# A two-layer decoder trunk in float32: the compressed branch's second products and two activation-table loads are issued elsewhere

## The chip, the cores and the metric

The kernel runs on one core of one Trainium2 chip. The metric is device time in microseconds (us) of one launch; the kernel before took 1310.82 us (median of three runs, 1310.17 to 1310.92). The core has five engines that work side by side, each through a queue of its own and in order: TensorE (PE in the profile; its weight loads are PEld), VectorE (DVE), ScalarE (ACT), GpSimd (POOL) and SyncE (SP), which here only issues DMAs.

## The reference, cut to what matters

Two layers, 512 tokens, width 1024, all float32. Layer 0 mixes by two linear recurrences, layer 1 by sparse attention with three branches; a SwiGLU network follows each. What the change touches is the compressed branch of layer 1 and the SiLU of the network:

```python
def compress_blocks(k, pos_emb, w1, w2):          # k: 512 tokens, 2 groups, 64 wide
    blocks = windows_of_32_tokens_every_16(k) + pos_emb      # 31 blocks
    return jax.nn.silu(blocks.reshape(..., 32 * 64) @ w1) @ w2   # 31 x 64 per group

def odd_mixer(h, ...):
    q, kc, vc, ks, vs, kw, vw, gl = split_cols(h @ w_in, ODD_COLS)
    k_cmp, v_cmp = compress_blocks(kc, ...), compress_blocks(vc, ...)
    # per head: softmax over k_cmp, over selected blocks and over a window;
    # the three outputs are mixed by sigmoid(gl), then h + out @ w_out

def swiglu(h, w_gate_up, w_down):
    g, u = jnp.split(h @ w_gate_up, 2, axis=-1)
    return (jax.nn.silu(g) * u) @ w_down
```

## The kernel before

Activations lie transposed: 8 tiles of 128 features by 512 tokens. Every large product is made of three matmuls (`mm3`, L89 to L91): operands are cut into a high part (a cast on ACT, L78: `wh`) and a low part (a subtraction, L79: `wl`, on DVE, or on POOL for the query weights). Weights come by DMA on SP's queue into `raw`, three buffers, in program order.

The program is written as a list of steps, and a scheduler with a simulated timeline turns it into one order for each engine; it keeps data dependences and buffer reuse, and moves instructions freely otherwise. `tc.issue_after(x)` tells it not to issue a step before instruction `x`; `tc.keep_in_program_order` keeps a step in its place among the others of its engine. The orders are fixed at build time: on the chip each engine takes its own strictly in turn and waits where an input is missing.

The stages that matter here, in order of time:

1. **The end of a layer's network** (`ffn`, L321 to L361). The hidden rows are made in groups of 2, 4, 4, 4, 4, 4. Each hidden tile goes through a SiLU on ACT (L343), a product on DVE (L344), and is cut into `hh` (ACT, L347) and `hl` (DVE, L348). Behind the loop ACT is told to load the table set that has both exp and ln (L355); then the last group's down projections follow.
2. **The head of layer 1** (`odd`, L705 on). Four projections (`proj`, tiles `ps_o`), the row norm (`row_rstd`: a matmul `ps_n`, then Ln on L127, Exp on L128, and three DVE steps L129 to L131), then for keys and values of the compressed branch `compress`: four DVE copies spread the projected tile `z` into `cx` (L832), eight fp32 matmuls with `w1` give `ps_c` (L837; the profile counts two passes for each), a short chain on ACT and DVE makes a SiLU out of exp, ln and exp (`sigmoid`, L152 to L156; result `cu`, L850), and the second product with `w2` gives `ps_c2` (L853 for keys, L858 for values). In the profile `ps_c` names both. Keys end up in `kc`, values in `vc`. The 96 matmuls of 304 columns into `ps_v` make the token-major values and the gates.
3. **Four query tiles** (`query_tile`, L782), 24 matmuls each into `ps_q`, scaled on DVE into `qz` (L798); then the attention loop, which first reads `kc` in `ps_cs` (L989).
4. **The head of layer 1's network**, the same code as stage 1 with `row_rstd` in the first hidden tile, and **the end** (`finish`): the final norm in two halves of 256 tokens, each with Ln and Exp (`rstd`), DVE products and output DMAs.

PSUM banks of tag `pt` go round in a ring of three: the first two projections, each `ps_c`, each `ps_c2` and the four early `ps_q` take them in program order.

Of the kernel before, what the change touches and what calls it, by code (L numbers as in the profile page):

```python
# [9 lines left out]
F32 = mybir.dt.float32  # L10
F32R = mybir.dt.float32r
U8 = mybir.dt.uint8
AF = mybir.ActivationFunctionType
# [23 lines left out]
AHEAD = 4  # L37
# [15 lines left out]
class Core:  # L53
# [216 lines left out]
    def ffn(self, outs, w_out, gain, layer, next_gain):  # L270
        tc, nc, io, sp = self.tc, self.nc, self.io, self.sp
        with tc.tile_pool(name="fs", bufs=1) as fs, tc.tile_pool(name="fps", bufs=6, space=PSUM) as fps:
            self.fs = fs
            acc = sp.tile([P, T], F32, tag="acc", name="acc", bufs=1)
            b = {i: [] for i in range(1, 8)}
            kept = []
            for i, m in enumerate(OUT_ORDER):
                ps = self.bank(self.turn + 1 + i // 3, "ps_o") if i in BANK_OUT else \
                    fps.tile([P, T], F32, tag="gu", name="ps_o")
                w = self.weight(w_out[m])  # L280
                if i == BANK_OUT[1] and self.last is not None:
                    with tc.issue_after(self.last):
                        self.dense_t(ps, w, outs)
                else:
                    self.dense_t(ps, w, outs)
                nc.vector.tensor_tensor(self.h[m], ps, self.h[m], ALU.add)
                self.token_side(m, gain, kept, b)
                self.square(m, self.h[m], acc)

            def product(i, a, ps=None):  # L290

                new = ps is None
                if new:
                    ps = fps.tile([P, T], F32, tag="gu", name=f"p{i}")[:, :TH]
                ah, al = a[i]
                for k, (bh, bl) in enumerate(b[i]):
                    c = slice(k * P, (k + 1) * P)
                    self.mm3(ps, ah[:, c], al[:, c], bh, bl, new and k == 0, k == 3, not new)
                return ps

            r = None
            out = []

            def down(hid, first, ms, last):

                nonlocal acc
                for m in ms:
                    ps = fps.tile([P, T], F32, tag="gu", name="ps_d") if last and m in OWN_DOWN else self.bank(m, "ps_d")
                    self.dense_t(ps, self.weight(io["dn"][layer, m, :, P * first:P * (first + len(hid))]), hid)
                    if last:  # L310
                        out.append(self.residual(m, ps, next_gain, acc))
                    else:
                        nc.vector.tensor_tensor(self.h[m], ps, self.h[m], ALU.add)  # L313


            before, first, done = None, 0, 0
            for size in GROUPS:
                hid = []
                for j in range(done, done + size):
                    a = self.weight_side(j, layer)  # L320
                    g = fs.tile([P, T], F32, tag="g", name="g", bufs=2)  # L321
                    s = fs.tile([P, T], F32, tag="s", name="s", bufs=2)
                    c1, c2, c3 = [fs.tile([P, TH], F32, tag="u", name="u", bufs=4) for _ in range(3)]


                    x = product(1, a)
                    nc.scalar.copy(c1, x)
                    y = product(5, a)
                    product(6, a, x)
                    nc.scalar.copy(c2, x)  # L330
                    nc.vector.tensor_tensor(g[:, :TH], product(2, a), c1, ALU.add)
                    if r is None:
                        r = self.row_rstd(acc, self.bank(1, "ps_n"))
                    product(7, a, x)
                    nc.scalar.copy(c3, x)
                    nc.vector.tensor_tensor(s[:, TH:], y, c3, ALU.add)  # L336
                    product(3, a, y)
                    nc.vector.tensor_tensor(g[:, TH:], y, c2, ALU.add)  # L338
                    product(4, a, x)
                    nc.vector.tensor_tensor(s[:, :TH], x, r[:, :TH], ALU.mult)  # L340
                    nc.gpsimd.tensor_tensor(s[:, TH:], s[:, TH:], r[:, TH:], ALU.mult)  # L341
                    (nc.vector if j == NF - 1 else nc.gpsimd).tensor_tensor(g, g, r, ALU.mult)  # L342
                    nc.scalar.activation(g, g, AF.Silu)  # L343
                    nc.vector.tensor_tensor(g, s, g, ALU.mult)  # L344
                    hh = sp.tile([P, T], F32R, tag="xh", name="hh", bufs=8)
                    hl = sp.tile([P, T], F32R, tag="xl", name="hl", bufs=8)
                    nc.scalar.copy(hh, g)  # L347
                    nc.vector.tensor_tensor(hl, g, hh.bitcast(F32), ALU.subtract)  # L348
                    hid.append((hh, hl))
                    if before:  # L350
                        n = KD // size
                        down(before, first, range((j - done) * n, (j - done + 1) * n), False)
                before, first = hid, done
                done += size
            tc.keep_in_program_order(nc.scalar.preload_act_table_set("natural_log_exp_and_others"))  # L355
            if next_gain is None:
                self.finish(hid, [io["dn"][layer, m, :, P * first:] for m in range(KD)], fps)
                return None, None
            acc = sp.tile([P, T], F32, tag="acc", name="acc", bufs=1)
            down(hid, first, range(KD), True)  # L360
            return out, acc  # L361
# [341 lines left out]
    def odd(self, xs, acc):  # L703
        tc, nc, io, sp = self.tc, self.nc, self.io, self.sp
        with tc.tile_pool(name="os", bufs=1) as os_, tc.tile_pool(name="ops", bufs=2, space=PSUM) as op:  # L705
# [3 lines left out]
            kc = os_.tile([P, 64], F32, name="kc")  # L709
# [16 lines left out]
            with tc.tile_pool(name="oe", bufs=1) as oe:  # L726
                self.oe = oe
                w1 = [oe.tile([P, 8, P], F32, tag="w1", name="w1", bufs=2) for _ in range(2)]
                w2 = oe.tile([64, 2, 64], F32, name="w2")
                for i in range(2):  # L730
                    nc.sync.dma_start(w1[i], io["w1"][i])
                nc.sync.dma_start(w2, io["w2"])
# [2 lines left out]
                r = self.row_rstd(acc, pn)  # L735
                pss += [proj(2), proj(3)]
                rt = self.token_rstd(r, op.tile([P, T], F32, tag="po", name="ps_rt", bufs=1))
                for col, ps in enumerate(pss):
                    z = oe.tile([P, T], F32, tag="z", name="z", bufs=3)
                    nc.vector.tensor_tensor(z, ps, r, ALU.mult)  # L740
                    if col < 2:
                        self.compress(col == 1, z, w1[col], w2, kc, vc)
                    else:
                        for g in range(2):
                            self.keys(z, g, *[a[:, col - 2] for a in kk[g]])
# [27 lines left out]
            with tc.tile_pool(name="ol", bufs=1) as ol_:  # L773
# [10 lines left out]
                def query_tile(step, late=True):  # L784

                    raw = raws.popleft()
                    w = self.split(raw, WN, True)
                    query_load()
                    yield
                    ps = self.bank(0, "ps_q") if late else op.tile([P, T], F32, tag="pt", name="ps_q", bufs=3)  # L790
                    for k, (xh, xl) in enumerate(xs):
                        wh, wl = w[k // 4]
                        c = slice(k % 4 * P, k % 4 * P + P)
                        self.mm3(ps, wh[:, c], wl[:, c], xh, xl, k == 0, k == 7)
                        if k % step == step - 1:
                            yield
                    z = ol_.tile([P, T], F32, tag="qz", name="qz", bufs=9)
                    nc.vector.scalar_tensor_tensor(z, ps, 0.125, r, ALU.mult, ALU.mult)  # L798
                    qz.append(z)
                    yield  # L800

                for _ in range(2):
                    query_load()
                for _ in range(AHEAD):
                    for _ in query_tile(1, False):
                        pass
                self.attention(qz, outs, kk, kc, vt, vc, v3, gates, query_tile)
                for i, o in enumerate(outs):
                    oh = sp.tile([P, T], F32R, tag="xh", name="oh", bufs=8)
# [12 lines left out]
        for o in (slice(0, 64), slice(64, P)):  # L822
            nc.vector.tensor_tensor(kl[o], z[own], kh.bitcast(F32)[own], ALU.subtract)

    def compress(self, is_v, z, w1, w2, kc, vc):
        nc, os_, op = self.nc, self.os, self.op
        i = int(is_v)
        x = self.oe.tile([P, 8, 66], F32, tag="cx", name="cx", bufs=1)
# [8 lines left out]
            nc.tensor.matmul(ps[:, :66], w1[:, m], x[:, m], start=m == 0, stop=m == 7)  # L837
        hi = os_.tile([64, 66], F32, tag="chi", name="chi", bufs=1)
        pc = os_.tile([64, 1], F32, tag="cpc", name="cpc", bufs=1)
        u = os_.tile([64, 2, 31], F32, tag="cu", name="cu", bufs=1)  # L840
        e = os_.tile([64, 2, 31], F32, tag="ce", name="ce", bufs=1)
        s = os_.tile([64, 2, 31], F32, tag="cs", name="cs", bufs=1)
        n = os_.tile([64, 2, 31], F32, tag="cn", name="cn", bufs=1)
# [4 lines left out]
        nc.vector.tensor_scalar(n, u, -1.0, None, ALU.mult)  # L848
        self.sigmoid(s, n, e)
        nc.vector.tensor_tensor(u, u, s, ALU.mult)  # L850
        ps2 = op.tile([P, T], F32, tag="pt", name="ps_c2", bufs=3)
        if not is_v:
            nc.tensor.matmul(ps2[:64, :62], w2[:, 0], u.rearrange("p g c -> p (g c)"), start=True, stop=True)  # L853
# [307 lines left out]
```

## Time and profile before

| | |
|---|---|
| median of the runs | 1310.82 us |
| the profiled execution's own time | 1311.86 us |
| its span, first to last instruction | 1308.9 us |
| PE busy | 1270.2 us (97%) |
| DVE, ACT, POOL busy | 79%, 56%, 25% |
| DMA | 115.10 MB, mean 88 GB/s |
| TensorE clock granted, mean | 0.984 of full |

How to read it: with PE at 97%, what can be gained lies where PE stands idle or runs at the lower clock. The profile's list of waits names these places, the timeline of one engine shows them in order, and the busy time by stretch gives the granted clock (1.00 is full, 0.50 is the lower level). A matmul's own duration includes its drain; the distance from one start to the next is its price in a row of matmuls.

### The profile page before, as it was taken

Reading aid. Unit: us, or ns where it says so; the run is one execution under the profiler, and the core shown is the slowest. Engines: PE = TensorE matmul, PEld = TensorE weight load, DVE = VectorE, ACT = ScalarE, POOL = GpSimd, SP = SyncE. Lnnn points to the kernel's source line nnn. Section 1 sums busy time; section 2 is a strip of 40 time slices with the busy share of each in tenths; the row PEclk is TensorE's granted clock in tenths of the full one; section 3 lists DMA queues with packets and bytes.
Section 4 is the critical chain, followed back from the end, with each engine's and each line's share of the span. In section 5 each row is a group of like instructions: output and inputs, shape, how many; then the busy total and the mean of one; then the engine's idle time right before and its main releaser. Section 6 shows DMA issues by size and latency. Waiting matters only on the chain.

```text
span 1308.9 us, 21707 instructions
## 1 busy us (share of the span) xinstructions
PE 1270.2 (97%) x7846; PEld 1120.7 (86%) x7846; DVE 1028.2 (79%) x2027; ACT 731.7 (56%) x1587; POOL 332.0 (25%) x371
## 2 busy tenths in 40 slices
PE   9999999998999999999988999999989999999995
PEld 7888888888999999999877888887889999999984
DVE  7896764699998887876762789995989888878755
ACT  6655444675554444444554778895755444444444
POOL 3432431001121111111015666762012111111101
PEclk9999999999999999999997999999989999999998
DMA  7212212123233333332322211101223333333321
GB/s 262 84 65 75 72 65 65 65 81 101 85 109 109 107 106 100 100 97 88 104 90 93 78 52 52 44 18 34 85 81 125 105 97 98 97 101 102 105 57 64
DMA packets 44123, 115.10 MB, mean 88 GB/s; under 512 B 4913, under 2 KB 10481, under 8 KB 44017
## 3 DMA queue, kind: packets, MB, share of 16 engines
q1 hardware_dynamic: 43872, 113.69, 27.2%
q8 instruction: 61, 1.00, 0.3%
q14 instruction: 46, 0.37, 0.1%
q10 hardware_dynamic: 144, 0.04, 0.0%
HBM read 111.62 MB, written 2.10 MB: 87 GB/s over the span
## 4 chain that ended last, share of the span: by engine, by line
PE 60%; DVE 8%; issue 2%; DMA 2%; ACT 2%; POOL 1%; DVEq 0%; ACTq 0%; POOLq 0%
PE p L89 9%; PE p L90 9%; PE p L91 9%; PE ps_d L90 5%; PE ps_d L91 5%; PE ps_d L89 5%; DMA raw<-in_gu 2%; PE po L966 2%; PE pt L935 2%; PE ps_o L89 2%; PE ps_o L91 2%; PE ps_o L90 2%; DVE wl L79 1%; PE ps_q L89 1%; PE ps_q L90 1%
## 5 line engine op out<-in xcount | busy, mean ns | idle before, releaser
L78 ACT CAST wh<-raw 128x512 fp32r<-128x512 f32 (+2 forms) x356 | 212.8, 605 | 216.2 <-PE p L90 76.8
L79 DVE TENSOR_TENSOR wl<-raw,wh 128x512 fp32r<-128x512 f32 (+2 forms) x340 | 244.0, 723 | 43.2 <-ACT wh L78 42.1
L214 ACT CAST sh<-sw 128x512 fp32r<-128x512 f32 x176 | 107.6, 618 | 144.4 <-PE p L90 126.4
L341 POOL TENSOR_TENSOR s<-s,rstd 128x256 f32<-128x256 f32 x44 | 38.9, 884 | 510.9 <-DVE s L336 451.7
L215 DVE TENSOR_TENSOR sl<-sw,sh 128x512 fp32r<-128x512 f32 x176 | 146.3, 848 | 6.5 <-ACT sh L214 6.2
L90 PE MATMUL ps_d<-hl,wh 128*128 128x512 f32 x344 | 136.0, 395 | 0.4 <-DVE hl L348 0.2
L91 PE MATMUL ps_d<-hh,wl 128*128 128x512 f32 x344 | 135.6, 394 | 0.0
L89 PE MATMUL ps_d<-hh,wh 128*128 128x512 f32 x344 | 134.5, 396 | 0.6 <-ACT hh L347 0.5
L342 POOL TENSOR_TENSOR g<-g,rstd 128x512 f32<-128x512 f32 x42 | 70.9, 1689 | 138.2 <-DVE g L338 114.5
L259 DVE TENSOR_TENSOR sw<-raw 128x512 f32<-128x512 f32 x44 | 30.3, 689 | 65.3 <-DMA raw<-in_gu 65.2
L91 PEld LDWEIGHTS ps_d<-hh,wl 128*128 128x128 f32 x344 | 64.5, 188 | 14.9
L918 ACT ACTIVATE p<-p,mx 128x256 f32<-128x256 f32 (+3 forms) x128 | 71.6, 564 | 10.1 <-DVE mx L910 9.6
L90 PE MATMUL ps_e<-xl,wh 128*128 128x512 f32 x192 | 76.7, 401 | 0.5 <-DVE xl L109 0.5
L927 POOL TENSOR_SCALAR p<-p,sm 128x128 f32<-128x128 f32 (+3 forms) x128 | 68.6, 554 | 33.2 <-DVE sm L924 15.0
L89 PE MATMUL ps_e<-xh,wh 128*128 128x512 f32 x192 | 76.8, 403 | 0.2
L91 PE MATMUL ps_e<-xh,wl 128*128 128x512 f32 x192 | 76.6, 401 | 0.0
L90 PEld LDWEIGHTS ps_d<-hl,wh 128*128 128x128 f32 x344 | 64.7, 188 | 13.2 <-DVE hl L348 1.0
L89 PEld LDWEIGHTS ps_d<-hh,wh 128*128 128x128 f32 x344 | 64.2, 188 | 13.5 <-ACT hh L347 1.0
L910 DVE CUSTOM_DVE_ANT_0 p<-ps_s,bias 128x256 f32<-128x256 f32 (+3 forms) x128 | 59.0, 481 | 8.1 <-PE pt L935 4.9
L313 DVE TENSOR_TENSOR h<-ps_d,h 128x512 f32<-128x512 f32 x80 | 54.6, 682 | 6.5 <-PE ps_d L91 6.3
L343 ACT ACTIVATE g<-g 128x512 f32<-128x512 f32 x44 | 27.8, 632 | 53.1 <-POOL g L342 52.9
L950 DVE TENSOR_TENSOR pl<-pt,ph 128x512 fp32r<-128x512 f32 (+2 forms) x96 | 51.5, 549 | 5.9 <-ACT ph L942 5.7
(342 smaller groups left out, 4112.8 us busy)
## 6 DMA issues: line engine op xcount, KB each, us to landing
raw<-in_gu SPq DMA_DIRECT2D x88, 512.0 KB, 3.8
raw<-in_dn SPq DMA_DIRECT2D x80, 256.0 KB, 2.7
raw<-in_ein SPq DMA_DIRECT2D x22, 512.0 KB, 3.7
raw<-in_oin SPq DMA_DIRECT2D x12, 512.0 KB, 3.7
raw<-in_eout SPq DMA_DIRECT2D x8, 512.0 KB, 3.8
bias<-in_bias SPq DMA_DIRECT2D x16, 256.0 KB, 2.6
raw<-in_oout SPq DMA_DIRECT2D x8, 512.0 KB, 3.5
h<-in_x SPq DMA_DIRECT2D x8, 256.0 KB, 5.0
```

Source lines behind the costliest of these rows:

```text
L78: nc.scalar.copy(wh[:, :m], raw[:, o:o + m])
L79: (nc.gpsimd if pool else nc.vector).tensor_tensor(wl[:, :m], raw[:, o:o + m], wh.bitcast(F32)[:, :m], ALU.subtract)
L89: mm(ps, ah, bh, start=start, stop=False, skip_group_check=more)
L90: mm(ps, ah, bl, start=False, stop=False, skip_group_check=more)
L91: return mm(ps, al, bh, start=False, stop=stop, skip_group_check=more)
L214: nc.scalar.copy(hi, src)
L215: nc.vector.tensor_tensor(lo, src, hi.bitcast(F32), ALU.subtract)
L313: nc.vector.tensor_tensor(self.h[m], ps, self.h[m], ALU.add)
L342: (nc.vector if j == NF - 1 else nc.gpsimd).tensor_tensor(g, g, r, ALU.mult)
L910: nc.vector.tensor_tensor_reduce(p, h["dst"][:, b - br[0]], h["bias"][:, T - n:], -1.0, 3e38, ALU.add, ALU.min, h["mx"][:, t, b:b + 1])
L918: nc.scalar.activation(p, p, AF.Exp, bias=h["mx"][:, t, b:b + 1], scale=-1.0, accum_out=h["sm"][:, t, b:b + 1])
L927: nc.gpsimd.tensor_scalar(p, p, h["sm"][:, t, b:b + 1], 1.0, ALU.mult, ALU.mult)
```

## The change

Two things are done. First, `compress` ends with `cu`; its second product, with all that follows (the copies into `kc`, the cuts and copies into `vc`), becomes `compress_out`, called for keys behind the first query tile and for values behind the second, each held with `issue_after` behind that tile's last matmul. `cu` gets two buffers, and `w2` moves to a pool that lives as long as needed. In program order the `pt` ring is now two projections, `ps_c`, `ps_c`, query tile 0, `ps_c2`, query tile 1, `ps_c2`, query tiles 2 and 3. Second, the table load behind each layer's network is held behind the last SiLU.

```diff
-                    nc.scalar.activation(g, g, AF.Silu)
+                    silu = nc.scalar.activation(g, g, AF.Silu).ins
...
-            tc.keep_in_program_order(nc.scalar.preload_act_table_set("natural_log_exp_and_others"))
+            with tc.issue_after(silu):
+                tc.keep_in_program_order(nc.scalar.preload_act_table_set("natural_log_exp_and_others"))
...
-                w2 = oe.tile([64, 2, 64], F32, name="w2")
+                w2 = os_.tile([64, 2, 64], F32, name="w2")
...
+                us = []
...
-                        self.compress(col == 1, z, w1[col], w2, kc, vc)
+                        us.append(self.compress(col == 1, z, w1[col]))
...
-                        self.mm3(ps, wh[:, c], wl[:, c], xh, xl, k == 0, k == 7)
+                        self.query_ins = self.mm3(ps, wh[:, c], wl[:, c], xh, xl, k == 0, k == 7).ins
...
-                for _ in range(AHEAD):
+                for i in range(AHEAD):
                     for _ in query_tile(1, False):
                         pass
+                    if i in (0, 1):
+
+                        with tc.issue_after(self.query_ins):
+                            self.compress_out(i == 1, us[i], w2, kc, vc)
...
-        u = os_.tile([64, 2, 31], F32, tag="cu", name="cu", bufs=1)
+        u = os_.tile([64, 2, 31], F32, tag="cu", name="cu", bufs=2)
...
         nc.vector.tensor_tensor(u, u, s, ALU.mult)
+        return u
+
+    def compress_out(self, is_v, u, w2, kc, vc):
+        nc, os_, op = self.nc, self.os, self.op
         ps2 = op.tile([P, T], F32, tag="pt", name="ps_c2", bufs=3)
```

What it does to the engines' orders (line numbers of the second of each pair are those of the changed kernel):

PE, the second product of the keys before, in the values' matmuls ahead of the query tiles (`w_7115` is `w2`, `w_7114` the values' `w1`):

```order
L90 MATMUL ps_v<-wl,xh 128x304
L91 MATMUL ps_v<-wh,xl 128x304
L853 MATMUL ps_c_7308<-cu,w_7115 64x62
L837 MATMUL ps_c<-cx,w_7114 128x66 x8
L89 MATMUL ps_v<-wh,xh 128x304
```

PE, the same product now, between query tiles 0 and 1:

```order
L90 MATMUL ps_q<-xl,wh 128x512
L91 MATMUL ps_q<-xh,wl 128x512
L863 MATMUL ps_c_7591<-cu,w_7115 64x62
L89 MATMUL ps_q<-xh,wh 128x512
L90 MATMUL ps_q<-xl,wh 128x512
```

It has moved behind the last 12 of the `ps_v` matmuls and 24 query matmuls; the values' second product has likewise moved from ahead of query tile 0 to behind query tile 1.

DVE, ahead of the values' first product, before (`kl` are low parts of keys, four of each pair of projections):

```order
L823 TENSOR_TENSOR kl_7104<-z,kh_7103 64x512 x2
L823 TENSOR_TENSOR kl_7106<-z,kh_7105 64x512 x2
L832 COPY cx<-z 64x8x32 x4
L845 TENSOR_TENSOR cpc<-ps_c,chi 64x1
L833 COPY cx<-par 128x8x2
L79 TENSOR_TENSOR wl<-raw,wh 128x304
```

DVE there now:

```order
L829 TENSOR_TENSOR kl_7104<-z,kh_7103 64x512 x2
L829 TENSOR_TENSOR kl_7106<-z,kh_7105 64x512
L838 COPY cx<-z 64x8x32 x4
L851 TENSOR_TENSOR cpc<-ps_c,chi 64x1
L839 COPY cx<-par 128x8x2
L829 TENSOR_TENSOR kl_7106<-z,kh_7105 64x512
L79 TENSOR_TENSOR wl<-raw,wh 128x304
```

One of the four subtractions has moved behind the copies. On PE the values' first product (L843) has gone with it: 36 `ps_v` matmuls now stand between the two first products, and 38 behind the second, where 63 and 12 stood.

ACT, the end of layer 1's network before:

```order
L355 ACT_TABLE_LOAD
L214 CAST sh<-sw 128x512
L335 COPY u<-p_14385 128x256
L78 CAST wh<-raw 128x512 x2
L327 COPY u<-p_14572 128x256
L78 CAST wh<-raw 128x512
L343 ACT_TABLE_LOAD
L343 ACTIVATE g<-g 128x512
L330 COPY u<-p_14385 128x256
L347 CAST hh<-g 128x512
```

ACT there now, with the last SiLU (the second `g<-g`):

```order
L343 ACTIVATE g<-g 128x512
L330 COPY u<-p_14572 128x256
L347 CAST hh<-g 128x512
L78 CAST wh<-raw 128x512 x2
L335 COPY u<-p_14572 128x256
L78 CAST wh<-raw 128x512 x2
L343 ACTIVATE g<-g 128x512
L356 ACT_TABLE_LOAD
L347 CAST hh<-g 128x512
```

Before, the load stood ahead of the last two SiLUs, which brought their own table back; each Ln and each Exp behind them in the program then had a load of its own. Now the load stands behind the last SiLU, and the Ln and Exp behind it have none: ACT's queue holds 5 table loads where it held 21. Up to the end of layer 0's network the orders are the same.

## Rows read from the trace of the kernel before

**Rows 1.** What PE waited for, whole span: us, times, longest

```profile
PE ps_c L853 <- DVE cu L850: 5.2, 1, 5.2
PE ps_c L858 <- DVE gates L767: 5.0, 1, 5.0
...
PE p L89 <- ACT t2h L214: 1.3, 1, 1.3
...
PE p L90 <- DVE t2l L215: 0.9, 1, 0.9
```

**Rows 2.** PE's timeline, layer 1's head: start, length, instruction, [idle before]

```profile
669.74 1.97 PE L837 MATMUL ps_c<-cx,w 128*128 128x66 f32 x16
...
680.54 0.30 PE L91 MATMUL ps_v<-wh,xl 128*128 128x304 f32 x1
686.04 0.47 PE L853 MATMUL ps_c<-cu,w 64*64 64x62 f32 x2 [5.20 <-DVE cu L850]
686.45 3.68 PE L837 MATMUL ps_c<-cx,w 128*128 128x66 f32 x16
...
698.25 0.60 PE L858 MATMUL ps_c<-w,cu 64*31 64x64 f32 x4 [4.99 <-DVE gates L767]
...
723.78 0.39 PE L902 MATMUL ps_s<-kh,q 128*128 128x512 f32 x1
```

**Rows 3.** Stretches: busy (count) PE, PEld, DVE, ACT, POOL; clock; DMA

```profile
672.00:681.00 9.00, 8.85 (x63) 8.60 (x63) 8.86 (x11) 4.61 (x9) 4.39 (x3) 1.00 0.17 58
...
686.00:693.00 7.00, 6.96 (x30) 6.73 (x30) 1.92 (x10) 3.22 (x11) 3.72 (x3) 0.50 0.44 149
...
704.00:724.00 20.00, 20.00 (x86) 16.11 (x85) 2.09 (x4) 4.49 (x8) 14.62 (x13) 0.99 0.23 79
```

**Rows 4.** ACT's timeline, layer 1's head

```profile
659.44 1.28 ACT L127 ACT_TABLE_LOAD   x1 [0.69 <-PE ps_n L135]
...
682.62 1.28 ACT L154 ACT_TABLE_LOAD   x1
683.92 0.26 ACT L154 ACTIVATE ce<-ce 64x62 f32<-64x62 f32 x1
```

**Rows 5.** DVE's timeline, layer 1's head

```profile
663.46 0.69 DVE L129 SCALAR_TENSOR_TENSOR rt<-rstd 128x512 f32<-128x512 f32 x1 [4.21 <-ACT rstd L128]
...
668.08 1.56 DVE L832 COPY cx<-z 64x256 f32<-64x256 f32 x4
...
673.70 3.79 DVE L823 TENSOR_TENSOR kl<-z,kh 64x512 fp32r<-64x512 f32 x4
677.50 3.54 DVE L832 COPY cx<-z 64x256 f32<-64x256 f32 x4
```

**Rows 6.** POOL's timeline, the same stretch: query weights' low parts

```profile
675.64 4.39 POOL L79 TENSOR_TENSOR wl<-raw,wh 128x512 fp32r<-128x512 f32 x3 [48.77 <-ACT wh L78]
```

**Rows 7.** SP's queue, 640 to 740: what its DMA issues waited for

```profile
SPq L889 <- DVE vw L764: 8.8, 1, 8.8
```

**Rows 8.** ACT's timeline, head of layer 1's network

```profile
947.12 1.28 ACT L128 ACT_TABLE_LOAD   x1
```

**Rows 9.** DVE's timeline, head of layer 1's network

```profile
949.08 0.69 DVE L129 SCALAR_TENSOR_TENSOR rt<-rstd 128x512 f32<-128x512 f32 x1 [1.34 <-ACT rstd L128]
```

**Rows 10.** A stretch of the network's head, columns as in Rows 3

```profile
953.50:960.20 6.70, 5.93 (x28) 5.64 (x27) 5.40 (x11) 2.40 (x5) 0.73 (x1) 0.50 0.51 179
```

**Rows 11.** ACT's timeline, last hidden tile of layer 1

```profile
1272.20 0.62 ACT L347 CAST hh<-g 128x512 fp32r<-128x512 f32 x1 [0.83 <-DVE g L344]
```

**Rows 12.** PE's timeline, the first matmuls that read it

```profile
1273.28 0.62 PE L89 MATMUL ps_d<-hh,wh 128*128 128x512 f32 x2
```

**Rows 13.** ACT's timeline, second half of the final norm

```profile
1298.68 1.28 ACT L128 ACT_TABLE_LOAD   x1
```

**Rows 14.** DVE's timeline, second half of the final norm

```profile
1298.80 0.41 DVE L399 TENSOR_TENSOR o<-h,r 128x256 f32<-128x256 f32 x1
1300.42 0.42 DVE L129 SCALAR_TENSOR_TENSOR rt<-r 128x256 f32<-128x256 f32 x1 [1.21 <-ACT r L128]
```

More of the change, by code (lines that the diff above doesn't have):

```diff
@@ L823, in keys, with compress @@
             nc.vector.tensor_tensor(kl[o], z[own], kh.bitcast(F32)[own], ALU.subtract)
-    def compress(self, is_v, z, w1, w2, kc, vc):
+    def compress(self, is_v, z, w1):
         nc, os_, op = self.nc, self.os, self.op
```

## The prediction, made before the changed kernel ran

> **What bounds the kernel now.** I read the list of PE's waits first, because PE is busy almost throughout and only what it does not do can be won. Two waits stand far above the rest, both at second products of the compressed branch: 5.2 us for the keys, 5.0 for the values [rows 1]. PE's own timeline shows that they are one place: from 680.54 on, the head of layer 1 stands still, does a few matmuls, stands still again, and attention opens at 723.78 [rows 2]. The busy time by stretch then shows a second loss that no list of waits has: behind the first wait the granted clock is 0.50, the lower of its two levels, 1.2 instead of 2.4 GHz, and it is back near full in the stretch from 704 [rows 3]. The same eight matmuls took 1.97 us ahead of the wait and 3.68 behind it [rows 2]. The wait for the values is put down to a `gates` step, which lies next to `cu` in DVE's queue; the matmul reads `cu`, so I take the chain behind `cu` as its cause: Exp, a table load, Ln, a table load, Exp, each load 1.28 us [rows 4].
>
> **The second products.** They are not removed, only moved to where `cu` is long done. What the place costs now is found best as a whole. From the end of the last matmul ahead of the wait (680.54 + 0.30 = 680.84) to the opening of attention at 723.78 are 42.94 us [rows 2]. The work in it, at full clock: the values' first product 1.97 [rows 2]; 12 `ps_v` matmuls at 8.85/63 = 0.14, 1.7 [rows 3]; the second products, 0.47 and 0.60 at the lower clock, so about 0.5 together [rows 2]; 96 query matmuls at 20.00/86 = 0.233, 22.3 [rows 3]. Sum 26.5, so 16.4 us are lost: 10.2 in the two waits, 6.2 through the clock. If PE is fed, all 16.4 come back, since attention's first inputs are ready before. What is late next? The bias tile's DMA waits on SP for the last cut of the values [rows 7], which follows `ps_v` and moves forward with it; the first `q` is made on POOL during query tiles 1 to 3. Inside the tiles DVE now carries the chain `qz`, `kc`, `qz`, `vc`: query tile 2 takes the bank that the `kc` copies free, tile 3 the one that `qz` of tile 1 frees, but a whole tile of 24 matmuls, 5.6 us, lies between each of these and its reader. Queued behind the `gates` steps, the first `qz` can be a little late without PE seeing it. I take nothing for it.
>
> **A new wait.** On PE the values' first product now stands 36 `ps_v` matmuls behind the keys': 669.74 + 1.97 + 36 x 0.14 = 676.7 [rows 2, 3]. It reads `cx`, which DVE filled from 677.50 [rows 5]. DVE's work there hangs on `rstd`, which came after two loads (the second, ahead of Exp, is as long as the one shown) [rows 4, 5]; without them DVE is 2.6 us earlier, and the one subtraction that moved behind the copies gives 3.79/4 = 0.9 more, so the copies start at about 674.0. They took 1.56 us for keys and 3.54 for values [rows 5], the latter beside POOL's subtractions at 4.39/3 = 1.46 each [rows 6]. Alone they end at 675.6, as now at 677.5, and behind three whole subtractions at 674.0 + 3 x 1.46 + 1.56 = 679.9. PE's wait is thus 0 to 3.2 us. I take 1.0, by the row of 3.54, since POOL starts its subtractions at about the same time as the copies; two short steps behind the copies are rounded in. The Trainium skill (SBUF — State Buffer, Who interferes with whom) says that a DVE copy in its two-port modes and a GpSimd instruction exclude each other, the later one standing for the whole of the other; the two copy rows agree in direction, and by the rule in full the upper end, 3.2, would hold, the sum being 2.2 smaller.
>
> **The table loads.** Sixteen loads vanish from ACT, most where ACT has time. On the path they count three times. In the head of layer 1 they feed the two parts above. In the head of layer 1's network the load ahead of Exp, 1.28 us, holds back ACT's cuts behind it [rows 8], and DVE stands 1.34 us for `rstd` [rows 9]; PE waits there for `t2h` and `t2l`, 2.2 us in all [rows 1]. `t2h` comes forward by the load, `t2l` by DVE's idle time, so PE gains 1.3; 0 if another input takes over, and up to 3.0 more if the clock stays up, because behind these waits 5.93 us of matmuls ran at 0.50 [rows 10]. I take 1.3: the other waits stay, and they sufficed for the drop to be likely. In the second half of the final norm two loads precede `r`, the second of them shown [rows 13], but DVE is free only at 1298.80 + 0.41 = 1299.21 and starts at 1300.42 [rows 14]: its 1.21 us of idle time are all that can go, 1.2.
>
> **The load behind the last SiLU.** ACT stood 0.83 us between the last SiLU and `hh` for DVE's product [rows 11]; a load of 1.28 there delays `hh` by 0.45. In layer 1 `hh` ends at 1272.82 and PE needs it at 1273.28 [rows 11, 12], so the delay just fits; `hl` follows and may miss by some tenths. I take a loss of 0.2 (0 to 0.5). In layer 0 PE has other down projections to do first. The Trainium skill (ScalarE: Activation LUTs, What ACT_TABLE_LOAD costs) gives 1283 ns for a load and about 1380 more for a drain at every change of set; here the next activation starts 0.02 us after its load [rows 4], so I see no drain. By the page this loss would be nearer 1.6 and the sum 1.4 smaller.
>
> **Sum.** 16.4 - 1.0 + 1.3 + 1.2 - 0.2 = 17.7 us. The profiled execution took 1311.86 us, of which 2.96 lie outside its span of 1308.9; that becomes 1294.2. It was 1.04 above the median of the runs, 1310.82, so I forecast 1293.1 for the median.
>
> **Rivals.**
> *A. The clock also recovers in the network's head.* If fewer waits there keep the full clock, 3.0 more come back [rows 10], and with no wait for `cx` 1.0 more: 1289.1. For it: one of PE's waits there nearly goes. Against: three shorter ones remain, and layer 0's head, which has no loads, looks much the same.
> *B. The first product of the values becomes the new stall.* The wait is 3.2 and the clock falls behind it as it did behind the 5.2; at a low stretch of some 7 us, as in [rows 10], that is 3.5 more. 6.7 instead of 1.0: 1298.8. For it: DVE has no idle time before these copies, and they slow down beside POOL.
> *C. Attention does not open earlier.* If the bias, the first `q` or the cut weights come when they come now, the 16.4 turns into one longer wait, and 1.3 + 1.2 - 0.2 remain: 1308.5. Against: all three hang on the values' cuts and the query tiles, which move forward.
> *D. Slower: the ring of banks makes the query tiles wait in turn.* A tile waits for a copy on DVE, this for ACT behind a cast that waits for PE. If PE is held 5 us at one of them and the clock is at its lower level for all 96 matmuls, this costs 22.3 + 5 against the 17.7 won: 1320.4. It decides when the bank of a tile is freed more than 5.6 us after the tile ahead of it began. The rows show no step that long.
> *E. The change does not do what it says*, a load or a wait being put back: the orders show neither, and I give it no chance of its own.
>
> **How the numbers follow.** Forecast 62%, A 15%, B 14%, C 6%, D 3%. The range leaves out C and D and takes in the bounds: low 16.4 + 1.3 + 3.0 + 1.2 = 21.9, so 1288.9; high is B with nothing won in the network's head, 1300.1, cut to 1299.5. A measurement of this kernel can tell about 0.2%, 2.6 us, from no change. Faster by more than that: forecast, A and B, 91%. Within it: C, 6%. Slower: D, 3%.
>
> **What would show it.** Right: PE's list of waits has no second product; attention opens at about 707 to 708; the clock is full from 666 to there; five table loads on ACT; `t2h` is no longer waited for; DVE's idle time before the last L129 is gone. Wrong: a wait over 2 us at the values' first product (L843), a stretch at 0.50 in the query tiles, a wait at the first `ps_s`, or `hh` late by a microsecond at either layer's end.

## The result, and the profile after

The changed kernel takes 1294.67 us (median of four runs, 1293.53 to 1295.57) against 1310.79 for the kernel before on the same chip: a ratio of 0.9877, 95% interval 0.986 to 0.9895. That is 16.1 us faster. Forecast were 1293.1, range 1288.9 to 1299.5. The profiled execution took 1294.29 us, 17.6 less than that of before, against 17.7 forecast; its span, 1292.3, is 16.6 less, and the other 1.0 lies outside the span, for which the forecast had no term.

PE's list of waits comes first again. It is the list of [rows 1], of the changed kernel (us in total, times, longest):

```profile
PE pn L388 <- DVE acc L121: 2.2, 1, 2.2
...
PE ps_c L843 <- DVE cx L839: 1.7, 1, 1.7
...
PE ps_d L90 <- DVE hl L348: 1.5, 2, 1.0
...
PE p L90 <- DVE t2l L215: 1.0, 1, 1.0
```

No second product (L863, L868) is in it, and no `t2h`. New are `cx` with 1.7 us and, in the network, a wait for `hl` of 1.0. PE's timeline at the head of layer 1, which answers to [rows 2]:

```profile
670.10 1.90 PE L843 MATMUL ps_c<-cx,w 128*128 128x66 f32 x16
...
676.71 0.30 PE L89 MATMUL ps_v<-wh,xh 128*128 128x304 f32 x1
678.70 2.00 PE L843 MATMUL ps_c<-cx,w 128*128 128x66 f32 x16 [1.69 <-DVE cx L839]
...
691.53 0.32 PE L863 MATMUL ps_c<-cu,w 64*64 64x62 f32 x2
...
697.57 0.41 PE L868 MATMUL ps_c<-w,cu 64*31 64x64 f32 x4
...
709.21 0.39 PE L912 MATMUL ps_s<-kh,q 128*128 128x512 f32 x1
```

Keys' first product, values' first product behind one wait, the two second products without any, attention. From the first to the last of these are 39.11 us; before it was 54.04 [rows 2]. The stretches show what else went. The column behind the five engines is the clock, and it never leaves 1.00, where before it was at 0.50 for a stretch [rows 3]:

```profile
672.00:681.00 9.00, 7.31 (x55) 7.07 (x55) 8.26 (x14) 3.24 (x8) 4.05 (x3) 1.00 0.21 63
686.00:693.00 7.00, 7.00 (x31) 5.39 (x31) 6.39 (x19) 5.37 (x18) 4.53 (x4) 1.00 0.26 91
697.00:709.00 12.00, 12.00 (x55) 9.39 (x54) 8.68 (x12) 2.78 (x5) 9.86 (x9) 1.00 0.29 88
```

All groups of ACT's table loads that are left (busy, mean ns):

```profile
L343 ACT ACT_TABLE_LOAD x2 | 2.6, 1283 | 0.0
L356 ACT ACT_TABLE_LOAD x2 | 2.6, 1283 | 0.0
L168 ACT ACT_TABLE_LOAD x1 | 1.3, 1283 | 0.7 <-PEq L1162 0.7
```

Five, one at the start and two for each layer's network.

A total hides which stage won what, so I cut every span at four rows of PE's timeline: the keys' first product, the first `ps_s` (attention opens), the first matmul on `t4h` (end of the head of layer 1's network) and the final norm's first `pn` on `acc`. Each row is one profiled execution, in us; the last column is the median of the kernel's runs:

| kernel | start to keys' product | to attention | to `t4h` | to `pn` | to the end | span | median |
|---|---|---|---|---|---|---|---|
| before | 669.74 | 54.04 | 232.63 | 333.64 | 18.85 | 1308.9 | 1310.79 |
| after | 670.10 | 39.11 | 232.08 | 334.76 | 16.25 | 1292.3 | 1294.67 |
| after, again | 671.35 | 39.12 | 228.69 | 332.75 | 16.29 | 1288.2 | 1293.61 |
| 1 loads only | 670.04 | 45.57 | 230.57 | 333.65 | 17.87 | 1297.7 | 1299.42 |
| 2 products only | 671.91 | 44.51 | 233.42 | 332.96 | 18.90 | 1301.7 | 1303.26 |
| 3 two `cx` | 670.24 | 37.16 | 230.65 | 334.47 | 17.78 | 1290.3 | 1293.85 |
| 4 POOL held | 671.42 | 37.15 | 231.04 | 335.74 | 17.85 | 1293.2 | 1291.36 |
| 5 loads only, PE filled | 669.07 | 42.80 | 230.90 | 334.47 | 16.26 | 1293.5 | 1296.16 |
| 6 two `cx`, tail filled | 670.77 | 37.16 | 229.27 | 333.04 | 16.26 | 1286.5 | 1289.38 |
| 7 load behind `hh` | 669.70 | 40.95 | 230.95 | 334.03 | 16.27 | 1291.9 | one run |
| 8 three edits | 671.17 | 37.31 | 229.01 | 334.25 | 16.26 | 1288.0 | 1289.49 |

The second row and the third are the same program. Their second and last columns agree within 0.04 us; the other three differ by 1.3, 3.4 and 2.0 from one execution to the next. So an effect of a microsecond is read in the column in which it arises, not from the span, and in the three noisy columns not from one profile.

### The profile page after: what moved, and what is told of

Its sections match the earlier page's. It is cut to its first block, busy times and chain, and to the rows that moved or that the text cites. A ratio compares the mean times of both kernels' runs of the same rounds, so it can differ in the third digit from the quotient of the medians.

```text
span 1292.3 us, 21693 instructions
## 1 busy us (share of the span) xinstructions
PE 1260.8 (98%) x7846; PEld 1111.7 (86%) x7846; DVE 1038.5 (80%) x2027; ACT 712.2 (55%) x1571; POOL 333.1 (26%) x371
## 4 chain that ended last, share of the span: by engine, by line
PE 58%; DVE 9%; DMA 3%; issue 2%; ACT 1%; POOL 1%; DVEq 0%; ACTq 0%; POOLq 0%; SPq 0%
PE p L89 8%; PE p L90 8%; PE p L91 8%; PE ps_d L90 5%; PE ps_d L91 5%; PE ps_d L89 5%; DMA raw<-in_gu 3%; PE po L976 2%; PE pt L945 2%; DVE wl L79 2%; PE ps_o L89 2%; PE ps_o L90 2%; PE ps_o L91 2%; PE ps_s L912 1%; PE ps_q L89 1%
## 5 line engine op out<-in xcount | busy, mean ns | idle before, releaser
L91 PEld LDWEIGHTS ps_d<-hh,wl 128*128 128x128 f32 x344 | 64.5, 188 | 14.9
```

Source lines behind the costliest of these rows:

```text
L91: return mm(ps, al, bh, start=False, stop=stop, skip_group_check=more)
```

## The experiments

**1 and 2: each half of the change alone.** The first keeps the second products where they were and queues the load of each layer's end behind the last SiLU. The second moves the products and leaves the load where it was.

The first, against the kernel before:

```diff
-            tc.keep_in_program_order(nc.scalar.preload_act_table_set("natural_log_exp_and_others"))
+            with tc.issue_after(silu): tc.keep_in_program_order(nc.scalar.preload_act_table_set("natural_log_exp_and_others"))
```

The second, against the changed kernel:

```diff
-            with tc.issue_after(silu):
-                tc.keep_in_program_order(nc.scalar.preload_act_table_set("natural_log_exp_and_others"))
+            tc.keep_in_program_order(nc.scalar.preload_act_table_set("natural_log_exp_and_others"))
```

> The kernel before with the table load of each layer's end behind the last SiLU; the second products stay where they were. Theory 1 (the two halves overlap): without its two loads each of the chains behind cu is 2.6 us shorter, and DVE also starts 2.6 earlier through rstd, so the keys' second product waits about 0.5 instead of 5.2, the values' 2 to 3 instead of 5.0, and the clock holds for most of the place. About 3 of the 16.4 us stay lost there; the network's head and the tail give 1 and 2.2 more: 1294.5 to 1296.5. Theory 2 (as the prediction booked it, the move earns the 16.4): each wait is shorter by its own two loads only, 2.6, and the clock still falls to 0.50: 5.2 + 1 + 2.2 won, 1302 to 1304.

> The changed kernel with the table load of each layer's end put back ahead of the last SiLU; the second products stay moved. 21 loads again. Theory 1: rstd is 2.6 us later, so DVE fills cx for the values 2.6 later while PE arrives when it did; the wait for cx at the values' first product is 3.5 to 4.5, the clock falls behind it, and of the 16.4 us 9 to 13 come back; network's head and tail as before: 1298 to 1302. Theory 2 (the move alone earns nearly all): the wait for cx is about 2, the clock holds, 1296 to 1297.

Measured: loads alone 1299.42 us, ratio 0.9919 (0.9904 to 0.9934); products alone 1303.26, 0.9944 (0.993 to 0.9957). Ahead of attention the loads alone win 54.04 - 45.57 = 8.5 us and the products alone 9.5, together 14.9. So the halves overlap by 3.1: both take from the same two stalls. The products alone stay above the ranges of both theories; the loads alone lie between the two, nearer to neither. In its rows the kernel with the products alone did what theory 1 says (a wait of 3.59, the clock down behind it, 9.5 won); it is 2.2 us behind before it gets to the keys' product, one of the three noisy columns. PE's timeline of the loads alone, and the stretch that begins at the second wait's end:

```profile
681.88 0.32 PE L853 MATMUL ps_c<-cu,w 64*64 64x62 f32 x2 [1.34 <-DVE cu L850]
...
690.15 0.60 PE L858 MATMUL ps_c<-w,cu 64*31 64x64 f32 x4 [4.31 <-DVE gates L767]
```

```profile
690.00:694.00 4.00, 3.85 (x12) 3.03 (x13) 3.46 (x19) 1.81 (x7) 0.00 (x0) 0.50 0.41 132
```

The keys' wait falls from 5.20 to 1.34, by more than the two loads in its own chain (2.56), because DVE too starts earlier. The values' wait falls by 0.7 only. DVE's first and last step of that chain, before and then here:

```profile
690.90 0.19 DVE L848 TENSOR_SCALAR cn<-cu 64x62 f32<-64x62 f32 x1
697.89 0.22 DVE L850 TENSOR_TENSOR cu<-cu,cs 64x62 f32<-64x62 f32 x1 [1.21 <-ACT cs L156]
```

```profile
685.26 0.27 DVE L848 TENSOR_SCALAR cn<-cu 64x62 f32<-64x62 f32 x1
689.79 0.22 DVE L850 TENSOR_TENSOR cu<-cu,cs 64x62 f32<-64x62 f32 x1
```

From the start of `cn` to the end of `cu` it took 7.21 us and takes 4.75, so it did get shorter by about its two loads, 2.46. But PE, at full clock here, does the values' first product and the 12 `ps_v` matmuls behind it in 3.7 us (682.13 to 685.84) where it took 6.8 (686.45 to 693.26), and so comes to the wait 1.8 us earlier in the course of the chain. The clock is lost at the second wait alone. Moving the products is what removes this one. And the products alone, where the loads keep `rstd` and with it `cx` late:

```profile
683.45 3.68 PE L843 MATMUL ps_c<-cx,w 128*128 128x66 f32 x16 [3.59 <-DVE cx L839]
```

```profile
683.50:687.50 4.00, 4.00 (x18) 4.00 (x19) 1.05 (x5) 3.01 (x4) 0.00 (x0) 0.50 0.66 238
687.50:691.50 4.00, 4.00 (x23) 4.00 (x23) 1.59 (x5) 2.37 (x7) 1.88 (x2) 0.74 0.26 74
```

This is rival B, in the kernel that lacks the loads' half: a wait of 3.59 at the values' first product, and the clock at 0.50 behind it.

**3 and 4: what the wait for `cx` is.** Two edits against the changed kernel: a second buffer for `cx`, which puts DVE's copies of the values right behind those of the keys, and on PE the values' first product right behind the keys'; or POOL's subtractions held back until the copies are done, with DVE's and PE's orders as they were.

The second buffer:

```diff
-        x = self.oe.tile([P, 8, 66], F32, tag="cx", name="cx", bufs=1)
+        x = self.oe.tile([P, 8, 66], F32, tag="cx", name="cx", bufs=2)
```

POOL held:

```diff
+                self.held = nc.gpsimd.tensor_copy(os_.tile([64, 32], F32, name="seen"), self.cx[64:, 7, 32:64]).ins
...
-                    w = self.split(raw, WN, True)
+                    with tc.issue_after(self.held): w = self.split(raw, WN, True)
```

> The changed kernel with two buffers for cx, so DVE copies the values' z behind the keys' copies, ahead of kl, and the values' first product stands right behind the keys'. Theory 1 (the wait of 1.69 for cx is DVE's order and nothing else is late behind it): no wait at that product, attention opens 1.7 us earlier, near 707.5, and the time is 1293.0. Theory 2: PE only meets the next late input (keys' low parts, casts of the query weights, the first q) and the time stays at 1294.7, within 0.5.

> The changed kernel with POOL's subtractions for the first query tiles queued behind a small copy that reads the last of the four copies into cx of the values; DVE's and PE's orders stay. Theory 1 (the copies are slow because POOL works beside them): four copies take about 1.6 us instead of 4.54, the wait for cx goes, POOL still ends before the first query tile, 1293.0. Theory 2 (the copies of the values are slow by themselves, or by something else): they stay at 3.5 to 4.5, the wait stays at 1.7, 1294.7.

Measured: 1293.85 us (ratio 0.9871, 0.9858 to 0.9883) and 1291.36 (0.9856, 0.9839 to 0.9872). Both open attention 37.15 us behind the keys' product, 1.96 earlier than the changed kernel, and PE waits for nothing on the way. The four copies of the values and POOL's work, first in the changed kernel, DVE and POOL:

```profile
673.84 4.54 DVE L838 COPY cx<-z 64x256 f32<-64x256 f32 x4
```

```profile
673.69 4.08 POOL L79 TENSOR_TENSOR wl<-raw,wh 128x512 fp32r<-128x512 f32 x3 [45.92 <-ACT wh L78]
```

then with POOL held, DVE and POOL:

```profile
675.16 1.56 DVE L838 COPY cx<-z 64x256 f32<-64x256 f32 x4
```

```profile
676.78 0.21 POOL L749 COPY seen<-cx 64x32 f32<-64x32 f32 x1 [47.68 <-DVE cx L838]
677.08 4.51 POOL L79 TENSOR_TENSOR wl<-raw,wh 128x512 fp32r<-128x512 f32 x3
```

Same copies, same place in DVE's queue: 4.54 us beside POOL, 1.56 alone. Theory 1 holds in both for this column. By their intervals the two medians are not told apart from the changed kernel's; the column tells them apart.

**5: what a wait costs beyond itself.** To the kernel of experiment 1 I add 18 matmuls on constants ahead of the values' second product, where PE stood for 4.31 us.

```diff
+        for _ in range(18 * is_v): nc.tensor.matmul(ps2[:62, 256:384], n.rearrange("p g c -> p (g c)"), self.ones[:64], start=True, stop=True)
```

(Two edges, which change no order, hold the query matmuls behind the second product.)

> The kernel with the loads moved and the products left (the first experiment), with 18 matmuls on constants added on PE right ahead of the values' second product, where PE waited 4.31 us; their results are not used. One takes about 0.21 us at full clock (half of 4.17/10 at the start of the trace), 3.8 in all. From the keys' first product to the opening of attention that kernel took 45.57 us, against 37.15 where PE waits for nothing: 1.34 + 4.31 of waits leave 2.8 that only the lower clock behind the long wait explains. Theory 1 (the wait lowers the clock): the second product comes no earlier, but the clock stays at 1.00 and the interval is 42.6 to 42.9, the time 1296.6. Theory 2 (the clock falls there for another reason, or the stretch has another bound): the interval stays at 45.3 or more and the time at 1299.4.

Measured: 42.80 us to attention and 1296.16 us (ratio 0.988, 0.9852 to 0.9908), as theory 1 has it. PE's timeline, and its stretches:

```profile
684.81 4.14 PE L852 MATMUL ps_c<-ones,cn 64*62 64x128 f32 x36
689.02 0.41 PE L859 MATMUL ps_c<-w,cu 64*31 64x64 f32 x4
```

```profile
684.80:689.00 4.20, 4.15 (x37) 3.90 (x36) 3.80 (x13) 2.94 (x12) 2.23 (x2) 1.00 0.48 160
689.00:693.00 4.00, 3.98 (x20) 3.20 (x21) 3.32 (x18) 2.41 (x8) 0.01 (x1) 1.00 0.45 136
```

(The trace counts one matmul on such data as two.) The work of the fill is useless and the second product needed the same data at the same point of the chain, yet 2.8 us come back: 0.16 ahead of that product, which starts 19.95 us behind the keys' first product instead of 20.11, and the rest behind it, where the clock now reads 1.00. They were the clock's share. There is one profile of each kernel here; that the clock fell by chance in the one without the fill is unlikely, since behind the other long waits, 5.20 us before and 3.59 in experiment 2, it reads 0.50 as well. The whole time is worth less as evidence: other columns moved too, the tail alone by 1.6.

**6: the same in the tail.** Against experiment 3: nine matmuls on constants ahead of the final norm's first `pn`, where PE waits 2.17 us for `acc`.

```diff
+            with tc.issue_after(end): [nc.tensor.matmul(pnf[:, TH:TH + P], self.ones, self.ones, start=True, stop=True) for _ in range(0 if half else 9)]
```

(One more edge keeps the second half's products behind that `pn`.)

> The kernel with two buffers for cx, with 9 matmuls on constants (about 1.9 us at full clock) on PE ahead of the first pn of the final norm, where PE waits 2.17 us for acc in every kernel so far; their results are not used. From that pn to the end of the span: 17.78 in the kernel this is made from, 17.87 and 17.85 in two others without loads there, all with the clock fallen behind the wait; 16.25 in the changed kernel's profile, where it happened to stay at 1.00. Theory 1 (the tail gained 2.6 instead of the 1.2 forecast because of the clock): the fill holds the clock and the interval is 16.2 to 16.5, the time 1292.4. Theory 2 (the 2.6 come from the loads of the first half, and DVE's chain bounds the tail whatever the clock): 17.6 to 17.9, time 1293.9.

Measured: 16.26 us from `pn` to the end and 1289.38 us (ratio 0.9837, 0.9813 to 0.9862). PE's timeline:

```profile
1267.90 2.17 PE L389 MATMUL pn<-ones 128*128 128x128 f32 x18
1270.24 0.70 PE L390 MATMUL pn<-acc,ones 128*128 128x256 f32 x2 [0.17 <-DVE acc L122]
```

With the clock up the tail is as short as theory 1 has it, here and again in experiment 8 (16.26 both times), and theory 2, a bound whatever the clock, falls. That the fill is what held the clock is not shown: four of the nine profiles without this fill kept it there too (16.25 to 16.29). The median is 4.5 us under that of experiment 3, where 1.5 were expected. The tail gave its 1.5; the profiles have the rest in the columns to `t4h` and to `pn`, which the edit does not touch and which differ as much between two executions of one program, but why the median is 3.0 lower is open.

**7: the price of the load behind the last SiLU.** Against the changed kernel, the load is queued behind the last `hh`.

```diff
-            with tc.issue_after(silu):
+            with tc.issue_after(last_hh):
```

> The changed kernel with the table load of each layer's end queued behind the last hh instead of the last SiLU. From the last SiLU to the first pn: 19.30 and 19.33 us in the two kernels with the load ahead of the SiLU, 19.63 to 19.67 in four with it between SiLU and hh. Theory 1 (the load is late for hh by about 0.45 and PE sees 0.33 of it): 19.3. Theory 2 (ACT is the bound there and the load only meets its next cast): 19.6 or more. The whole time is too close to tell: 1294.3 by theory 1, 1294.7 by theory 2.

Measured, one run, 1293.85 us. ACT's timeline in the changed kernel, then here:

```profile
1256.42 0.63 ACT L343 ACTIVATE g<-g 128x512 f32<-128x512 f32 x1
1257.07 1.28 ACT L356 ACT_TABLE_LOAD   x1
1258.36 0.62 ACT L347 CAST hh<-g 128x512 fp32r<-128x512 f32 x1
```

```profile
1256.34 0.63 ACT L343 ACTIVATE g<-g 128x512 f32<-128x512 f32 x1
1257.79 0.62 ACT L347 CAST hh<-g 128x512 fp32r<-128x512 f32 x1 [0.83 <-DVE g L344]
1258.43 1.28 ACT L356 ACT_TABLE_LOAD   x1
```

From SiLU to `pn`: 1276.05 - 1256.42 = 19.63 us, and 1275.63 - 1256.34 = 19.29 with the load behind `hh`. So the load costs 0.33, theory 1; the kernel of experiment 8 has 19.30 again. Something I had not looked for stands in the second column: 40.95 instead of 39.11. The wait for `cx` is 1.80 here instead of 1.69, but this time the clock fell behind it (PE's stretches):

```profile
677.70:681.70 4.00, 2.74 (x17) 2.74 (x18) 2.52 (x11) 1.30 (x5) 0.08 (x1) 0.80 0.36 106
681.70:685.70 4.00, 4.00 (x24) 4.00 (x24) 1.87 (x5) 1.21 (x4) 2.02 (x2) 0.77 0.79 286
```

**8: the three edits together, beside the changed kernel on one chip.** Two `cx`, the tail's fill and the load behind `hh`.

> The changed kernel with the three edits together: two buffers for cx, 9 matmuls on constants ahead of the final norm's first pn (their results are not used), and the load of each layer's end behind the last hh. If the three stretches do not touch each other: 37.15 us from the keys' first product to attention, 19.3 from the last SiLU to the pn less nothing for the fill, 16.26 from the pn to the end; against the changed kernel 1.96 + 0.33 and, where its clock falls in the tail, 1.5: 1.9 to 3.8 us under it. If they do (the load behind hh also changes the order at layer 0's end, where it could cost the first part), the gain is under 1.5.

> The changed kernel once more, on the same chip as the kernel with the three edits. In its first profile the clock stayed full behind the 2.17 us wait of the final norm, and fell there in three of the five other profiles without loads and fill. If that is chance from run to run, pn to end is 16.3 or 17.8 here with the same program; its median should lie at 1294 to 1296, and the kernel with three edits 2 to 4 us under it.

Measured: 1289.49 us (1286.61 to 1290.09; ratio 0.9832, 0.9817 to 0.9847) against 1293.61 for the changed kernel (1291.77 to 1295.17; 0.9872, 0.9857 to 0.9887). That is 4.1 less, a little over the 1.9 to 3.8 expected. The changed kernel's median lies a little under the 1294 to 1296 expected, and its tail kept the clock again, 16.29. The stretches are as expected: 37.31, 19.30 and 16.26. So a faster version than both kernels exists, at about 1289.4, with (8) or without (6) the move of the load.

## Why the prediction was right, point by point

| step | forecast | measured |
|---|---|---|
| second products, PE fed | 16.4 | 54.04 - 37.15 = 16.9 |
| wait for `cx` | -1.0 | 37.15 - 39.11 = -1.96 |
| head of the network | +1.3 | +1.0; +2.4 in the second profile |
| tail | +1.2 | +2.6: loads 1.1, clock 1.5 |
| load behind the last SiLU | -0.2 | -0.33 in layer 1 |
| not in the sum: start, attention, rest of the network | 0 | -0.4, -0.4, -0.8; -1.6, +1.5, +1.2 |
| sum for the span | 17.7 | 16.6; 20.7 |

(Where two values stand, the second is of the changed kernel's second profile; its span compares with the one profile of before. The rows of the network are from `ps_n` to `t4h` and from there to the last SiLU.)

That the sum came so close is partly luck: 1.0 too little taken off at `cx`, 0.3 too much hoped for in the network's head, 0.1 at the load and 1.6 in the stretches left out stand against 0.5 more from the second products and 1.4 more in the tail. The second profile of the same program gives 20.7. What was right is the mechanism of the main term: of the first profile's 16.6, 14.9 arose ahead of attention.

**The second products.** Where PE is fed, experiments 3, 4 and 6, the place takes 37.15 to 37.16 and the gain is 16.9, 0.5 more than forecast. Of the 16.9, 10.2 are the two waits, which leaves 6.7 where 6.2 were booked for the clock. That such a remainder is the clock experiment 5 shows on the smaller one of experiment 1, 2.8; for the 6.7 the rows show the clock at 0.50 from 684 to 704, and no run gives it back alone. What was too simple is that I booked the term to the move. The loads alone bring 8.5 of it, and neither half gets to 14.9 alone. The forecast was for both and so did not suffer. The `gates` in [rows 1] were rightly not taken for the cause. The chain behind `cu` is: without its two loads it is 2.5 us shorter (experiment 1), and the wait shrinks less only because PE gets to it sooner.

**The wait for `cx`.** This term was mis-sized, 1.0 against 1.96. The copies started at 673.84, forecast 674.0; PE was there at 677.01, forecast 676.7. What failed is the choice of the row of 3.54 for their duration: it had a later start against POOL, and here, side by side with POOL from the start, the four took 4.54, as of three copies of 1.4 and one of 0.37. The rest, 0.27, is no wait that the list shows: the list counts from the end of the last `ps_v` matmul, 677.01, while in a row the next would have started 0.14 behind its start, at 676.85, and the product itself took 2.00 instead of 1.90. The Trainium skill (SBUF — State Buffer, Who interferes with whom) says that a DVE copy in its two-port modes and a GpSimd instruction exclude each other, and the later one stands for the whole of the other. Experiment 4 agrees in kind, 4.54 against 1.56; whether these copies run in such a mode no row shows. The upper end as I had worked it out, three whole subtractions plus all copies, 3.2, was too much by 1.5.

**The head of layer 1's network.** `t2h` is gone from the list as forecast, `t2l` stays with 1.00 us. PE's rows, before and then in the changed kernel:

```profile
944.83 1.02 PE L135 MATMUL ps_n<-acc,ones 128*128 128x512 f32 x2
951.70 0.38 PE L90 MATMUL p<-t2l,sh 128*128 128x256 f32 x1 [0.88 <-DVE t2l L215]
```

```profile
930.71 1.02 PE L135 MATMUL ps_n<-acc,ones 128*128 128x512 f32 x2
936.23 0.39 PE L90 MATMUL p<-t2l,sh 128*128 128x256 f32 x1 [1.00 <-DVE t2l L215]
```

From `ps_n` to the matmul on `t2l` were 6.87 us and are 5.52. So `t2l` did come forward by DVE's idle time, 1.3 as forecast, and PE still waits for it because it is there 1.3 earlier too, without the wait for `t2h`. Of this 0.35 is lost again ahead of `t4h`, where in this profile the clock fell sooner than before. The 0 to 3.0 that I had put down as bounds by the clock vary between executions of one program. The same stretch in the first and in the second profile of the changed kernel, PE's clock in the third column from the end:

```profile
932.00:946.00 14.00, 10.63 (x72) 9.72 (x71) 12.85 (x27) 7.83 (x18) 1.31 (x1) 0.88 0.28 95
```

```profile
930.00:944.00 14.00, 10.91 (x79) 9.56 (x78) 13.21 (x28) 8.00 (x18) 0.74 (x1) 1.00 0.28 95
```

So the clock's recovery, rival A's main part, happens in some executions and not in others: of the nine profiles without loads five have the clock at 1.00 through this stretch (the second of the changed kernel, experiments 1, 3, 6 and 8). The gain up to `t4h` was 2.4 then, not the 1.3 + 3.0 of rival A; the lower stretch before reaches beyond `t4h`. Part of the gain here is given back soon behind it. A wait for `hl` of 0.7 to 1.0 us, about 22 us later, is in seven of the nine profiles without loads; before has none there, experiment 2 one of 0.34. In the changed kernel DVE stood there for a weight's DMA:

```profile
959.69 0.69 DVE L259 TENSOR_TENSOR sw<-raw 128x512 f32<-128x512 f32 x1 [1.12 <-DMA raw<-in_gu]
```

That `hl` is late through this row is read from the queue's order and was not tried.

**The tail.** The term for the loads was right. The rows of PE at which the norm's halves begin, before and then in the changed kernel:

```profile
1290.05 0.70 PE L387 MATMUL pn<-acc,ones 128*128 128x256 f32 x2 [2.17 <-DVE acc L121]
1295.80 0.59 PE L387 MATMUL pn<-acc,ones 128*128 128x256 f32 x2
```

```profile
1276.05 0.70 PE L388 MATMUL pn<-acc,ones 128*128 128x256 f32 x2 [2.17 <-DVE acc L121]
1280.28 0.59 PE L388 MATMUL pn<-acc,ones 128*128 128x256 f32 x2
```

From the second half's `pn` to the end took 13.10 us before and 13.12 in experiment 2, which has the loads, and takes 12.0 to 12.1 in all nine profiles without them: 1.1, where 1.2 were forecast, and DVE's last L129, at 1283.84, has no idle time ahead of it. The first half's loads were rightly taken for hidden: from the first `pn` to the second took 5.75 and 5.78 us with them, and 5.68 to 5.81 without them in experiments 1, 3 and 4; in all five the clock fell there. What the forecast lacked is a term for the clock, which it put at nothing. Where it stays up, that stretch takes 4.14 to 4.23, and this is the other 1.5 of the 2.6. The changed kernel got them by chance as far as the runs show: three kernels with the same tail and no loads lost the clock there.

**The load behind the last SiLU.** 0.33 by experiment 7, inside the forecast's 0 to 0.5. In layer 0 it costs next to nothing: from the last SiLU to the keys' first product are 46.44 us with it (670.10 - 623.66), 46.50 before (669.74 - 623.24) and 46.30 with the load behind `hh` (experiments 7 and 8). The Trainium skill (ScalarE: Activation LUTs, What ACT_TABLE_LOAD costs) would add some 1.38 us of drain; `hh` starts 0.01 us after the load ends, and no run shows a drain.

**The rivals.** C and D fell: attention opened early and the query tiles never waited. B did not occur in the changed kernel but did in experiment 2, with 3.59 and 3.8 where 3.2 and 3.5 were priced. The signs came as listed except for the opening of attention, at 709.2 instead of 707 to 708, by the 0.36 that the head began late and the 1.0 more at `cx`. (By the forecast's own terms it should have said 708.4: 723.78 less 16.4 plus 1.0.)

## What to carry to other kernels

A stall of PE is priced as the whole interval from the last matmul ahead of it to the next stage, less the work at full clock; the list of waits shows only part of it. Where a wait cannot be removed, work put into it can save the part that the clock would take: matmuls on constants gave back 2.8 us behind a wait of 4.31 (experiment 5). Real work in their place was not tried. Two edits that shorten the same chain are to be tried alone and together, since what each brings depends on the other.

## What the runs showed of the hardware that I had not expected

What a wait costs through the clock is not in proportion to it in these profiles, one for each row but the last. In the stretch from the keys' first product to attention, against 37.15 us without waits:

| kernel | PE's waits | lost in all | left over |
|---|---|---|---|
| before | 5.20 + 4.99 | 16.89 | 6.7 |
| 1 loads only | 1.34 + 4.31 | 8.42 | 2.8 |
| 2 products only | 3.59 | 7.36 | 3.8 |
| 7 load behind `hh` | 1.80 | 3.80 | 2.0 |
| after, both profiles | 1.69, 1.70 | 1.96, 1.97 | 0.3, 0.3 |

Where the rows show the lower level, what is left over is the clock's, less some 0.2 of the kind counted at `cx` above. They show it behind 3.59, 4.31 and 5.20, where before it lasts through the wait of 4.99, and behind 1.80. Behind 1.69 and 1.70 they show none, and the 0.3 there is not the clock's. And of nine profiles with the same 2.17 at the final norm's `pn`, five lost the clock behind it (before and experiments 1 to 4) and four kept it (the changed kernel twice, 5 and 7), though the tail of 3 and 4 is the same program as that of the changed kernel. What decides there is open.
